# Score products of a head pair as 64-row products, with the operand B | K stored once and without zeros

## The chip, the cores and the metric

The kernel runs on one core of one Trainium2 chip. The metric is the device time of one execution in microseconds (us), taken as the median of several runs. The time before is 2406.82 us, the median of three runs (2398.74 to 2412.68).

## What is computed

One inference step of a two-layer decoder trunk: 1024 prompt tokens and 8 x 8 sample tokens, 1024 channels. Layer 0 is an HGRN2 recurrence, layer 1 an RWKV-7 recurrence; both have a memory cross-attention, a gate and an output projection. The change lies in layer 1. There, for each of 16 heads with 64 channels, the reference runs this over the tokens:

```python
def step(S, inp):
    r_t, w_t, k_t, v_t, a_t, b_t = inp
    sa = jnp.einsum('bhij,bhj->bhi', S, a_t)
    S = S * w_t[:, :, None, :] + sa[..., None] * b_t[:, :, None, :] + v_t[..., None] * k_t[:, :, None, :]
    y = jnp.einsum('bhij,bhj->bhi', S, r_t)
    return S, y
```

The kernel does it in chunks of 64 tokens. Within a chunk it needs all products of a row of B or K (with their decays, written B~ and K~) with a column of A or R (A~, R~): the scores, a 128 x 128 matrix for each head and chunk, which a mask then makes triangular.

## The kernel before

**Blocks.** Layer 1's tokens form nine blocks of the class `Blk`: eight of 128 prompt tokens (two chunks, E = 2) and one of the 64 sample tokens (E = 1); their order is RSEQ = 0, 8, 1, 2, ... (L32), so the sample block is the second. A block's 16 heads are 8 pairs. A pair owns 128 channels, which lie on the 128 partitions: head h of it on the half `HV[h]` (partitions 0 to 63, or 64 to 127). Four pairs form a group k, of which there are two.

**The parts of a block**, each a method, in the order in which a block goes through them:
- `pre` (L1399), per group: loads sg, kk, bb, k2 and r by DMA on SP's queue, a running sum G on DVE (L1425), two exponentials on ACT (L1427, L1428), then B~ | K~ into `BKz` by four products: K~ on POOL (L1432) and B~ on DVE (L1435), each once for each head, on that head's 64 partitions. A~ | R~ are made on POOL (L1440 to L1442) into `AR`.
- `score_steps` (L1457), per group, chunk and head: four products (pairs j) on TensorE into one PSUM bank `psc` (L1471), with `BKz` as the weights and `AR` as what streams; DVE multiplies the bank by the mask into `Q` (L1474). Every such product is fp32, and the trace shows it as two instructions.
- `tokens` (L1481): B~ | K~ transposed to tokens on partitions (L1499), per group and head, one instruction per chunk and pair, and a copy by ACT (L1305).
- `inverse` (L1516): a substitution on DVE in 15 steps (L1544, L1545) between copies on ACT (L1535) and DVE transposes; `merge_steps` (L1555): 32 x 32 products on TensorE (L1570) with copies on ACT and DVE.
- `chain` (L1631): the recurrence itself, with products at L1660, L1662, L1687, L1701 and L1710 (for the sample block L1657 in place of L1660); `sample_in` (L1616, products L1612 and L1627) and `sample_out` (L1746) move the sample states, `out_group` (L1776) normalises the result.

`BKz` is one tile of [128, 2 (head), 4, 4, 64] for each group (L945), made once. Channels of the other head in it are zero, set once by POOL (L948). So a product with it runs over all 128 partitions, and the zeros keep the other head's channels out. There is one `BKz` per group for all blocks: the next block's `pre` can write it when this block's `score` and `tokens` have read it.

**Banks.** `psc`, the transposes' `pbk` and (at the end) `pf` share the two banks of the pool `psm` (L1195). The merge has two banks of its own, the chain three.

**Order.** The lists PLAN and PLAN2 (L43) put the parts of the first two blocks among the last gates (products `pg`) and the memory attention. Then the loop at L1263 runs for each block n: chain(n) with high priority; values(n + 1); the merge of block n + 1 and the score of block n + 2 woven by `weave` (L1310) with `WV = (1, 2)`: one step of the merge, two of the score (one bank each), in turn; tokens and inverse of n + 2; pre of n + 3; out of n - 1. The framework then orders each engine's instructions itself, by an estimate of their times (`schedule_with_timeline_sim=True`, L1859), within what the data and priorities allow. On the chip each engine takes its instructions in the order thus fixed, so one that waits holds up those behind it.

Of the kernel before, what the change touches and what calls it, by code (L numbers as in the profile page):

```python
# [34 lines left out]
# buffers of the memory attention's tiles, by layer  # L35
XB = [2, 2]
OWB = 5
# pool of each tag of the recurrence's tiles; the others lie with the temporaries
WHERE = dict(s="s", ec="a", ecs="a", S0="l", S1="l", yv="l", o4="l", Q0="q", Q1="q", BK0="b", BK1="b")
WHERE |= {t: "t" for t in ("Ld", "Lu", "L16", "pd", "XN", "XP", "XM")}  # L40
# order of the last gates, the memory attention and the first parts of the recurrence
# [6 lines left out]
WV = (1, 2)  # L48
# [5 lines left out]
RB1 = dict(s=5, AR=6, Q=6, BKt=5, BKts=2, UV=3, UVs=2, XN=1, XP=1, W=3, S0=2, S1=2, yv=3, o4=3, ec=6, ecs=2, Sn0=2)  # L54
BF = dict(hs=3, oT=3, q=3, zn=3, lt=2, B=2, W=5, qe=1, ke=1, vv=3, cmp=2, eb=2, kt=1, S=6, oi=1, kts=1, S0=2, vx=1)
EV = 5
# banks in the heads: projections, memory attention, levels, other products of the prompt, of the sample
# [3 lines left out]
# order of the branch's channel tiles in the output projection  # L61
# [21 lines left out]
def setup(ctx, tc, g):  # L83
# [23 lines left out]
    # channel vectors as columns: [128, 128] = 16 vectors x 8 channel tiles  # L107
# [25 lines left out]
    # the token before the samples' first, as columns (batch, channel tile)  # L133
# [17 lines left out]
def sigmoid_ps(g, s, ps):  # L151
    """s = 1 / (1 + exp(-ps)) through exp and log."""
    nc = g.nc
    nc.scalar.activation(s, ps, AF.Exp, scale=-1.0)
    nc.vector.tensor_scalar(s, s, LNTOP, None, op0=ALU.min)
    nc.scalar.activation(s, s, AF.Ln, bias=1.0)
    nc.scalar.activation(s, s, AF.Exp, scale=-1.0)
# [7 lines left out]
def rstd_of(g, ss, n, scale, eps, p=128, sm=None):  # L165
    """(ss * scale + eps) ** -0.5 for a [p, n] tile."""
# [15 lines left out]
def norm_rows(g, xs, x, p):  # L182
    """xs = RMS-normalised rows (without the gain) of x [p, D]."""
# [16 lines left out]
def load_w(g, pool, src, w, kt=KT, elo="pool", raws=2):  # L200
    """hi/lo parts of src [kt * 128, w]."""
# [16 lines left out]
def gemm_cm(g, w, xh, xl, pieces, evac, m=128, c0=0):  # L218
    """out[c, t] = sum_k w[k, c] x[k, t], c on partitions; evac(ps, t0, n) per piece."""
# [10 lines left out]
def gemm_ko(g, w, xh, xl, evac):  # L230
    """As gemm_cm over all tokens, with the contraction outermost."""
# [12 lines left out]
def build_hT(g, xsrc, layer, hi, lo, sp):  # L244
    """Normed, transposed rows of the residual, as hi/lo parts [128, KT, T]."""
# [20 lines left out]
def memory_kv(g, mp, sp, kT0, v0):  # L266
    """Keys kT [128 d, XH, MEM] and values v [128 m, 2, 512] of the memory for both layers; the second's go to g.kv1.

    Also writes the two cache outputs.
    """  # L270
# [45 lines left out]
def softmax_rows(g, pool, ps, nblk, layer, rowmask=None):  # L316
    """softmax(QS * s) over the last axis of ps [128, nblk, MEM] -> SBUF tile."""
# [19 lines left out]
def cross_prompt(g, pool, q, h, kT, v, o, layer):  # L337
    """o [128, 256] = attention of head h over the memory; q [128, 256] queries."""
# [17 lines left out]
class Cross:  # L356
    """Memory attention of one layer into rows D.. of mixT, in parts: head(h) for the prompt, then sample(b) per batch."""
# [23 lines left out]
    def sample(self, bs, sp):  # L381
        """Batches bs of one group; the heads lie on the quadrants, four batches (32 tokens) form a group."""
# [70 lines left out]
def batch_masks(g):  # L453
    """bmask[(h, t32), bb] = (t32 // 8 == bb); blk[t, b] = (t mod 64 // 8 == b)."""
# [13 lines left out]
def hgrn_layer(ctx, g):  # L468
# [13 lines left out]
    # values, tokens on partitions  # L482
# [15 lines left out]
    with pool(g, "xk", 1, "right") as xk:  # L498
# [7 lines left out]
        with pool(g, "hm", 1, "right") as hm, pool(g, "h2", 1, "right") as h2, pool(g, "xc", 1, "right") as xc, \  # L506
# [13 lines left out]
            def gate(j, ms):  # L520
                """Rows 128 j.. of the branch, ms (two tiles by tokens), times silu of their gate."""
# [58 lines left out]
def hgrn_head(g, hd, wp, xh, xl, h2, hq, mbase, mlev, smask, att, atts, oT):  # L580
    """A head in two halves of the prompt's tokens, the second with the sample's."""
# [9 lines left out]
    # q = silu(z)  # L591
# [9 lines left out]
    # lt = -log f, f = sigmoid(z) (one HGRN2 layer: its lower bound lbs[0] - lbs[0] is zero)  # L601
# [20 lines left out]
def hgrn_half(g, hd, half, h2, own, mbase, mlev, smask, q, zn, lt, vv, att, atts, oT, S):  # L622
# [4 lines left out]
    # k = 1 - f = exp(zn - lt)  # L627
# [6 lines left out]
    # B = -cumulative log decay within the chunk  # L634
    B = own("B", "B")[:, :N]
    nc.vector.tensor_tensor_scan(B, smask[:, 512 * half:512 * half + N], lt, 0.0, op0=ALU.mult, op1=ALU.add)
    # two-token blocks
# [65 lines left out]
    # inter-chunk operands: qe = q exp(b), ke = k exp(b_last - b)  # L703
# [42 lines left out]
    # sample: eight batches of eight tokens  # L746
# [30 lines left out]
def hgrn_norm_out(g, h2, po, n, p, dst):  # L777
    """RMS norm over the head's value channels, then transposed into dst [128, n * p]."""
# [14 lines left out]
class NextNorm:  # L793
    """Rows of the second layer's normed input, transposed as they are made."""
# [40 lines left out]
def load_out_w(g, layer, pl, raws, ks):  # L835
    """hi/lo parts of rows of the output projection, through the pools of raws in turn."""
# [13 lines left out]
class BranchTile:  # L850
    """Gated branch of a row tile, hi/lo."""
# [21 lines left out]
def out_proj(g, layer, ws, orp, orb, done, first=None, xp=None):  # L873
    """Residual + gated branch @ w_out, rows of 128 tokens; done(i, p, x, xs) takes each row tile.

    The first layer's runs one tile later; what the last one takes is returned, its rows in pool xp.
    """
# [39 lines left out]
def rwkv_masks(g, rc, c):  # L917
    """Masks over [(s of either operand), columns of a chunk]: s < t for those of A~, s <= t for those of R~; others."""
# [18 lines left out]
    # 0 where a run of decays starts, for the scans over (pair, token)  # L937
# [6 lines left out]
    # B~ | K~ of each head, 0 in the other head's channels; per group of four pairs  # L944
    g.BKz = [rc.tile([128, 2, 4, 4, 64], F32, name=f"BKz{k}") for k in range(2)]  # L945
    for k in range(2):
        for h in range(2):
            nc.gpsimd.memset(g.BKz[k][HV[1 - h], h], 0.0)  # L948
    # inverse: identities, the lower left 16-blocks, and which 16-block a row belongs to
# [33 lines left out]
def rwkv_layer(ctx, g, nn, left):  # L983
# [13 lines left out]
    # the operands' ring of 11 slots; three of them outlive it  # L997
# [359 lines left out]


def bonus(g, pr, r, slot_):
    """Bonus weights r . (rk k) per token and head."""  # L1360
    nc = g.nc
    k2 = slot_("k2")
    nc.sync.dma_start(out=k2, in_=g.k2T[128 * pr:128 * pr + 128, :])
# [499 lines left out]
```

## Time and profile before

| | us |
|---|---|
| median of three runs | 2406.82 (2398.74 to 2412.68) |
| profiled execution, first to last instruction (span) | 2406.3 |
| mean granted TensorE clock in it | 0.942 of full speed |
| first and last score product (psc) | 1657.3 and 2137.7 |
| first and last chain product L1660 | 1804.2 and 2232.6 |

The profile gives the profiled execution by its span; no time beyond the span is listed for it. Engines are PE (TensorE products), PEld (its weight loads), DVE (VectorE), ACT (ScalarE), POOL (GpSimd), SP (SyncE, which issues DMAs). PEclk is the clock granted to TensorE as a share of full speed; its two levels are 2.4 GHz (1.0) and 1.2 GHz (0.5). "Busy" of PE counts modelled durations that overlap, so 94% busy is not 94% of what it could do. A row "x16" of the timeline merges 16 instructions of one line that follow one another; the time beside it runs from the first one's start to the last one's end.

### The profile page before, as it was taken

What the parts mean: (1) busy time and instruction counts of PE and PEld (TensorE: products, weight loads), DVE (VectorE), ACT (ScalarE), POOL (GpSimd) and SP (SyncE); (2) the same over time, 40 slices, a digit from 0 to 9 for tenths busy, and PEclk for the clock granted to TensorE, in tenths of its full rate; (3) what the DMA queues carried; (4) which work ended last, traced back from release to release, by engine and by line L of the source; (5) the groups of instructions that cost most, each with busy time, mean ns of one, the idle gap of its engine ahead of it and who ended that gap; (6) DMA issues with size and microseconds to landing.
All of it is one profiled execution on the core that took longest, in us unless ns stands there. A gap on an engine that the chain in (4) does not pass through costs nothing. (4 is left out here: it accounts for less than half of the span.)

```text
span 2406.3 us, 51073 instructions
## 1 busy us (share of the span) xinstructions
PE 2207.1 (92%) x20980; PEld 1975.4 (82%) x20981; DVE 1448.3 (60%) x2729; ACT 1080.7 (45%) x2384; POOL 947.9 (39%) x783
## 2 busy tenths in 40 slices
PE   5988999999999888997988999899999989999997
PEld 5988888877777776887988999788898978888776
DVE  6213686686788855347588403235568589795643
ACT  4223565555555543238455422344544455454421
POOL 2113564463566530013455422112224265545442
PEclk9998999999998999999999999999988799898999
DMA  5334111221443136314334343325533224323653
GB/s 183 84 95 145 37 56 49 71 62 39 105 116 108 55 108 192 115 40 166 137 128 147 122 134 115 92 58 118 153 107 95 72 79 112 88 69 94 194 161 106
DMA packets 360315, 253.02 MB, mean 105 GB/s; under 512 B 120378, under 2 KB 326402, under 8 KB 360082
## 3 DMA queue, kind: packets, MB, share of 16 engines
q1 hardware_dynamic: 348034, 237.66, 33.2%
q0 software_dynamic: 2544, 7.64, 1.0%
q10 hardware_dynamic: 9504, 4.46, 0.7%
q8 instruction: 165, 2.70, 0.5%
q14 instruction: 68, 0.56, 0.1%
HBM read 172.59 MB, written 77.11 MB: 104 GB/s over the span
## 5 line engine op out<-in xcount | busy, mean ns | idle before, releaser
L197 POOL TENSOR_TENSOR wlo<-wraw,whi 128x1024 fp32r<-128x1024 f32 (+1 forms) x84 | 217.8, 2595 | 435.5 <-ACT whi L194 421.9
L213 PE MATMUL pg<-hi,whi 128*128 128x288 f32 (+3 forms) x800 | 271.2, 339 | 13.3 <-DVE gs L532 9.3
L215 PE MATMUL pg<-hi,wlo 128*128 128x288 f32 (+3 forms) x800 | 268.1, 335 | 0.0
L214 PE MATMUL pg<-lo,whi 128*128 128x288 f32 (+3 forms) x800 | 267.1, 334 | 0.0
L213 PEld LDWEIGHTS pg<-hi,whi 128*128 128x128 f32 x800 | 156.9, 196 | 27.5 <-DVE gs L532 10.2
L194 ACT ACTIVATE whi<-wraw 128x1024 fp32r<-128x1024 f32 (+1 forms) x92 | 100.9, 1098 | 161.5 <-issue 88.4
L214 PEld LDWEIGHTS pg<-lo,whi 128*128 128x128 f32 x800 | 156.5, 196 | 12.0 <-issue 2.8
L215 PEld LDWEIGHTS pg<-hi,wlo 128*128 128x128 f32 x800 | 156.6, 196 | 11.4 <-issue 1.7
L900 PE MATMUL pout<-owh,bh 128*128 128x512 f32 (+1 forms) x432 | 142.8, 398 | 14.9 <-ACT owh L194 14.6
L900 PE MATMUL pout<-owl,bh 128*128 128x512 f32 (+1 forms) x432 | 141.5, 393 | 0.0
L900 PE MATMUL pout<-owh,bl 128*128 128x512 f32 (+1 forms) x432 | 141.0, 394 | 0.5 <-DVE bl L197 0.5
L213 PE MATMUL pg<-xhi,whi 128*128 128x384 f32 (+2 forms) x392 | 127.9, 326 | 5.7 <-DVE evs L1146 2.8
L671 POOL TENSOR_TENSOR W<-W,zn 128x256 f32<-128x256 f32 (+1 forms) x96 | 91.7, 955 | 90.2 <-ACT W L670 81.6
L215 PE MATMUL pg<-xhi,wlo 128*128 128x384 f32 (+2 forms) x392 | 126.2, 322 | 0.0
L214 PE MATMUL pg<-xlo,whi 128*128 128x384 f32 (+2 forms) x392 | 125.6, 320 | 0.0
L900 PEld LDWEIGHTS pout<-owh,bh 128*128 128x128 f32 (+1 forms) x432 | 78.8, 183 | 36.6 <-ACT owh L194 15.9
L194 ACT ACTIVATE bh<-br 128x512 fp32r<-128x512 f32 (+1 forms) x54 | 31.9, 605 | 166.0 <-POOL br L869 82.6
L197 DVE TENSOR_TENSOR bl<-br,bh 128x512 fp32r<-128x512 f32 (+1 forms) x54 | 47.1, 873 | 97.4 <-ACT bh L194 97.4
L239 PE MATMUL pg<-xhi,wlo 128*128 128x384 f32 (+1 forms) x408 | 97.2, 335 | 0.0
L900 PEld LDWEIGHTS pout<-owh,bl 128*128 128x128 f32 (+1 forms) x432 | 78.6, 182 | 21.9 <-DVE bl L197 0.9
L900 PEld LDWEIGHTS pout<-owl,bh 128*128 128x128 f32 (+1 forms) x432 | 78.9, 183 | 20.8 <-issue 0.4
L1471 PE MATMUL psc<-AR,BKz 128*128 128x128 f32 x544 | 85.6, 314 | 11.1 <-DVE Q L1474 11.1
(474 smaller groups left out, 6508.8 us busy)
## 6 DMA issues: line engine op xcount, KB each, us to landing
wraw<-in_w_in_dram SPq DMA_DIRECT2D x72, 512.0 KB
oraw<-in_w_out_dram SPq DMA_DIRECT2D x24, 512.0 KB
wraw<-in_w_mem_kv_dram SPq DMA_DIRECT2D x16, 512.0 KB
gT<-evs SPq DMA_DIRECT2D x12, 544.0 KB
vv<-vtk SPq DMA_DIRECT2D x24, 256.0 KB
br<-brT SPq DMA_DIRECT2D x24, 256.0 KB
gt<-gT SPq DMA_DIRECT2D x24, 256.0 KB
br<-mixT SPq DMA_DIRECT2D x24, 256.0 KB
```

The source lines that it names most:

```text
L194: nc.scalar.activation(hi, src, AF.Copy)
L197: (nc.gpsimd if elo == "pool" else nc.vector).tensor_sub(lo, src, hi.bitcast(F32))
L213: nc.tensor.matmul(out, ah, bh, start=first, stop=False)
L214: nc.tensor.matmul(out, ah, bl, start=False, stop=False)
L215: nc.tensor.matmul(out, al, bh, start=False, stop=last)
L239: nc.tensor.matmul(z[:, :n], a[:, k], x(k)[:, t0:t0 + n], start=first, stop=last)
L671: nc.gpsimd.tensor_mul(Wv[:, :, 0, :], Wv[:, :, 0, :], kv[:, :, 0, :])
L900: nc.tensor.matmul(ps[c][:p], a[:, k, :p], w[:, 512 * c:512 * c + 512], start=first, stop=last)
L1471: nc.tensor.matmul(ps[:, j], two(BK[:, h, j, 2 * e:2 * e + 2]), two(AR[:, j, 2 * e:2 * e + 2]), start=True, stop=True)
```

## The change

The tile of zeros is gone. B~ | K~ of a group is a tile `BK` of [128, 4, 4, 64] with each head on its own half of the partitions, and each block takes a new one: two buffers per group, `BKc0` and `BKc1`, in the pool that held `BKz` (4 x 4 KB per partition in place of 2 x 8 KB). Both heads of a group are written by one instruction on 128 partitions. A score step takes both banks at once: for each pair j the two heads' products run on partitions 0 to 63 and 64 to 127, into a bank for each head, then both masks follow. There are half as many steps, and `weave` takes one of each kind in turn. The transposes take a pair's 128 channels at once, with a bank per chunk in place of one per head. The diff also removes comments and docstrings, which are left out here.

```diff
-WHERE = dict(s="s", ec="a", ...
+WHERE = dict(BKc0="s", BKc1="s", s="s", ec="a", ...
-WV = (1, 2)
+WV = (1, 1)
-RB1 = dict(s=5, AR=6, ...
+RB1 = dict(BKc0=2, BKc1=2, s=5, AR=6, ...
...
-    g.BKz = [rc.tile([128, 2, 4, 4, 64], F32, name=f"BKz{k}") for k in range(2)]
-    for k in range(2):
-        for h in range(2):
-            nc.gpsimd.memset(g.BKz[k][HV[1 - h], h], 0.0)
...
-        BK = g.BKz[k]
+        BK = self.tile("BK", f"BKc{k}", 4, 4, 64)
+        self.BK.append(BK)
...
-        for h in range(2):
-            getattr(nc, ENG["bk0"]).tensor_mul(BK[HV[h], h, :, ri, :], v4(k2)[HV[h]], v4(En)[HV[h]])
+        getattr(nc, ENG["bk0"]).tensor_mul(BK[:, :, ri, :], v4(k2), v4(En))
         r = ld(g.rTr, "r")
-        for h in range(2):
-            getattr(nc, ENG["bk1"]).tensor_mul(BK[HV[h], h, :, ai, :], v4(bb)[HV[h]], v4(En)[HV[h]])
+        getattr(nc, ENG["bk1"]).tensor_mul(BK[:, :, ai, :], v4(bb), v4(En))
...
             for e in range(E):
+                zs = [g.psm.tile([128, 4, 128], F32, name="psc", tag="m") for _ in range(2)]
+                for j in range(4):
+                    for h in range(2):
+                        nc.tensor.matmul(zs[h][:, j], two(BK[HV[h], j, 2 * e:2 * e + 2]), two(AR[HV[h], j, 2 * e:2 * e + 2]),
+                                         start=True, stop=True)
+                m = g.rmask_s if self.sample else g.rmask[:, self.turn(e, k)]
                 for h in range(2):
-                    ps = g.psm.tile([128, 4, 128], F32, name="psc", tag="m")
-                    for j in range(4):
-                        nc.tensor.matmul(ps[:, j], two(BK[:, h, j, 2 * e:2 * e + 2]), two(AR[:, j, 2 * e:2 * e + 2]),
-                                         start=True, stop=True)
-                    m = g.rmask_s if self.sample else g.rmask[:, self.turn(e, k)]
-                    nc.vector.tensor_tensor(Q[:, e, h], ps, m[:, None].to_broadcast([128, 4, 128]), op=ALU.mult)
-                    yield
+                    nc.vector.tensor_tensor(Q[:, e, h], zs[h], m[:, None].to_broadcast([128, 4, 128]), op=ALU.mult)
+                yield
...
-            for h in range(2):
-                ps = g.psm.tile([128, E, 4, 64], F32, name="pbk", tag="m")
-                for e in range(E):
-                    for j in range(4):
-                        nc.tensor.transpose(ps[:, e, j], two(BK[HV[h], h, j, 2 * e:2 * e + 2]), g.ident[HV[h], HV[h]])
-                copy(nc, ENG["bkt"], BKt[:, :, :, HV[h]], ps)
+            for e in range(E):
+                ps = g.psm.tile([128, 4, 128], F32, name="pbk", tag="m")
+                for j in range(4):
+                    nc.tensor.transpose(ps[:, j], two(BK[:, j, 2 * e:2 * e + 2]), g.ident)
+                copy(nc, ENG["bkt"], BKt[:, e], ps)
```

## Rows read from the trace of the kernel before

**Rows 1.** The page's busy time of each engine: us, share of the span, instructions.

```profile
PE 2207.1 (92%) x20980; PEld 1975.4 (82%) x20981; DVE 1448.3 (60%) x2729; ACT 1080.7 (45%) x2384; POOL 947.9 (39%) x783
```

**Rows 2.** The table by stretches of layer 1's end: stretch in us from the span's start, its length, busy us of PE, PEld, DVE, ACT and POOL (instructions), granted clock, DMA share, GB/s.

```profile
1650.00:1790.00 140.00, 133.04 (x1319) 124.27 (x1318) 80.36 (x152) 68.25 (x158) 40.06 (x41) 0.94 0.46 129
1790.00:1930.00 140.00, 135.31 (x1922) 126.49 (x1921) 100.11 (x192) 68.19 (x165) 52.08 (x50) 0.78 0.32 83
1930.00:2070.00 140.00, 125.12 (x2186) 110.54 (x2185) 125.73 (x232) 69.51 (x174) 81.74 (x80) 0.92 0.37 97
2070.00:2170.00 100.00, 96.43 (x1680) 84.13 (x1677) 88.19 (x173) 51.71 (x135) 53.84 (x56) 0.94 0.29 76
```

**Rows 3.** The chain of waits by line, each a share of its stretch. The first row is the stretch from 1640 to 2260 us (620 us); the others are 1790 to 1930, 1930 to 2070 and 2070 to 2170 us. The rows end where the view cuts them.

```profile
by line: PE psc L1471 8.7%; PE py L1570 6.3%; PE chain L1662 5.4%; PE pn L1570 5.3%; DVE pd L1544 4.6%; PE chain L1660 4.0%; PE chain L1687 3.8%; PE pg L213 3.7%; PE pg L215 3.7%; PE pg L214 3.6%; DVE BKz L1435 3.4%; issue 2.9%; PE chain L1
...
by line: PE psc L1471 16.0%; PE pas L1627 10.0%; DVE pd L1544 8.0%; PE py L1570 6.7%; PE pn L1570 6.6%; PE chain L1662 5.5%; DVE BKz L1435 4.2%; PE chain L1657 3.6%; PE px L1570 3.3%; DVE Xc L1545 3.3%; PE pbk L1499 2.8%; DVE G L1425 2.6%; 
...
by line: DVE pd L1544 8.8%; PE py L1570 7.8%; PE psc L1471 7.1%; DVE BKz L1435 6.8%; PE chain L1660 6.5%; PE chain L1662 6.5%; issue 5.2%; PE pn L1570 5.1%; PE chain L1687 3.9%; DVE bx L1758 3.6%; ACT Ld L1535 3.4%; DVE N1p L1583 3.1%; DVE 
...
by line: PE psc L1471 12.5%; PE chain L1687 9.7%; PE py L1570 8.8%; PE chain L1662 8.8%; PE chain L1660 7.8%; PE chain L1701 7.1%; PE pn L1570 6.1%; PE chainS L1710 5.0%; DVE pd L1544 4.5%; PE px L1570 4.3%; PE pec L1767 4.2%; PE pbk L1499 
```

**Rows 4.** The instructions that write or read the banks psc: count, duration in ns (least, median, most), first and last start in us, shapes (rows*columns of weights, what streams).

```profile
L1471 PE MATMUL psc<-AR,BKz x544: 270/275/582, 1657.5 to 2137.7; 128*128 128x128 f32 x182
L1474 DVE TENSOR_TENSOR Q<-psc,rm x64: 636/682/693, 1665.7 to 2140.1; 128x512 f32<-128x512 f32 x64
L1474 DVE TENSOR_TENSOR Q<-psc,rms x4: 680/691/692, 1787.7 to 1792.2; 128x512 f32<-128x512 f32 x4
```

**Rows 5.** The score products alone (L1471) by the same stretches: length, busy us of PE and of PEld (instructions), granted clock, DMA share, GB/s; below, their sum over 600 us.

```profile
1790.00:1930.00 140.00, 34.94 (x203) 30.90 (x201) 0.78 0.32 83
...
sum 600.00, PE 85.63 PEld 76.37; mean PE 17.13 PEld 15.27
```

**Rows 6.** Score products in the timeline: start in us, us, engine, line, count [idle before, and who ended it]. The first stretch ran at half clock, the second at full clock.

```profile
1853.78 3.79 PE L1471 MATMUL psc<-AR,BKz 128*128 128x128 f32 x16 [0.81 <-DVE Q L1474]
...
1860.33 2.05 PE L1471 MATMUL psc<-AR,BKz 128*128 128x128 f32 x16
```

**Rows 7.** The timeline again, products on halves of the array at full clock: transposes of 64 rows in a prompt block (eight of one head in turn) and in the sample block (four of each head), the chain's L1710 (two columns' halves in turn) and its L1701 (one column half).

```profile
1994.05 0.71 PE L1499 MATMUL pbk<-ident,BKz 64*128 64x64 f32 x8 [0.32 <-ACT BKt L1305]
...
1794.95 0.47 PE L1499 MATMUL pbk<-ident,BKz 64*128 64x64 f32 x8
...
1797.67 0.47 PE L1499 MATMUL pbk<-ident,BKz 64*128 64x64 f32 x8
...
2142.64 0.69 PE L1710 MATMUL chainS<-UV,BKt 128*64 128x64 f32 x16
...
1867.77 1.15 PE L1701 MATMUL chain<-UV,Q 128*64 128x64 f32 x16
```

**Rows 8.** The instructions that write or read BKz and AR, columns as in Rows 4.

```profile
L1499 PE MATMUL pbk<-ident,BKz x272: 221/223/364, 1687.3 to 2153.6; 64*128 64x64 f32 x136
L1435 DVE TENSOR_TENSOR BKz<-bb,sg x36: 404/773/1774, 1513.2 to 2115.0; 64x512 f32<-64x512 f32 x32, 64x256 f32<-64x256 f32 x4
L1432 POOL TENSOR_TENSOR BKz<-k,sg x36: 722/1352/1772, 1514.0 to 2114.5; 64x512 f32<-64x512 f32 x32, 64x256 f32<-64x256 f32 x4
L948 POOL MEMSET BKz<- x4: 947/950/1116, 1484.0 to 1487.0; 64x1024 f32 x4
...
L1442 POOL TENSOR_TENSOR AR<-r,G x18: 739/1270/1724, 1652.7 to 2120.9; 128x512 f32<-128x512 f32 x16, 128x256 f32<-128x256 f32 x2
```

**Rows 9.** The timeline of DVE, and of POOL below, at 1847 to 1856 us.

```profile
1848.92 1.21 DVE L1544 TENSOR_TENSOR pd<-Xc,L 128x81 f32<-128x81 f32 x1
...
1853.95 0.31 DVE L1544 TENSOR_TENSOR pd<-Xc,L 128x144 f32<-128x144 f32 x1
...
1846.57 3.45 POOL L1432 TENSOR_TENSOR BKz<-k,sg 64x512 f32<-64x512 f32 x2 [4.90 <-ACT sg L1427]
1850.10 1.25 POOL L1440 TENSOR_TENSOR AR<-kk,G 128x504 f32<-128x504 f32 x1
```

**Rows 10.** A transpose of 128 rows in the timeline, at full clock.

```profile
2239.31 0.66 PE L1739 MATMUL pf<-ident,S 128*128 128x128 f32 x4 [0.28 <-POOL S L1716]
```

**Rows 11.** Who waited for whom from 1640 to 2260 us: us in total, times, the longest.

```profile
POOL BKz L1432 <- PE pbk L1499: 23.5, 7, 8.7
...
PE psc L1471 <- DVE Q L1474: 11.1, 5, 3.5
```

**Rows 12.** Who waited for the instructions on BKz (us, times), of the view of that tile.

```profile
  DVE BKz L1435: 4.3, 2
```

**Rows 13.** Four stretches of the sample block's stage, columns as in Rows 2.

```profile
1815.00:1835.00 20.00, 18.86 (x302) 17.36 (x302) 17.93 (x33) 10.80 (x26) 11.34 (x14) 1.00 0.29 80
1835.00:1859.00 24.00, 23.19 (x236) 21.94 (x234) 20.35 (x41) 9.49 (x23) 9.81 (x8) 0.51 0.33 89
1859.00:1876.00 17.00, 17.00 (x298) 15.76 (x297) 11.06 (x17) 11.83 (x28) 5.74 (x6) 0.99 0.32 80
1876.00:1896.00 20.00, 20.00 (x231) 18.87 (x231) 12.85 (x34) 6.67 (x16) 3.65 (x3) 0.51 0.31 80
```

More of the change, by code (lines that the diff above doesn't have):

```diff
@@ L37 @@
 OWB = 5
-WHERE = dict(s="s", ec="a", ecs="a", S0="l", S1="l", yv="l", o4="l", Q0="q", Q1="q", BK0="b", BK1="b")
+WHERE = dict(BKc0="s", BKc1="s", s="s", ec="a", ecs="a", S0="l", S1="l", yv="l", o4="l", Q0="q", Q1="q", BK0="b", BK1="b")
 WHERE |= {t: "t" for t in ("Ld", "Lu", "L16", "pd", "XN", "XP", "XM")}
@@ L53 @@
 GQ = ()
-RB1 = dict(s=5, AR=6, Q=6, BKt=5, BKts=2, UV=3, UVs=2, XN=1, XP=1, W=3, S0=2, S1=2, yv=3, o4=3, ec=6, ecs=2, Sn0=2)
+RB1 = dict(BKc0=2, BKc1=2, s=5, AR=6, Q=6, BKt=5, BKts=2, UV=3, UVs=2, XN=1, XP=1, W=3, S0=2, S1=2, yv=3, o4=3, ec=6, ecs=2, Sn0=2)
 BF = dict(hs=3, oT=3, q=3, zn=3, lt=2, B=2, W=5, qe=1, ke=1, vv=3, cmp=2, eb=2, kt=1, S=6, oi=1, kts=1, S0=2, vx=1)
@@ L1399, in pre @@
     def pre(self):
-        self.AR, self.ec = [], []
+        self.AR, self.BK, self.ec = [], [], []
         for k in range(2):
@@ L1463, in score_steps @@
         for k in range(2):
-            AR, BK = self.AR[k], g.BKz[k]
+            AR, BK = self.AR[k], self.BK[k]
             Q = self.tile("Q", f"Q{(2 * self.at + k) % 6}", 2, 2, 4, 128)
@@ L1487, in tokens @@
         for k in range(2):
-            BK = g.BKz[k]
+            BK = self.BK[k]
             if (self.i, k) == (7, 1):
```

## The prediction

> **What bounds the kernel now.** I read the page first: PE is busy 92% of the span, DVE 60%, POOL 39% [rows 1], so the question is what PE does where the change acts. All instructions on BKz and psc lie between the first pre and the last score at 2138 us, the products from 1657 us on [rows 4, 8]; so I cut that part into stretches. The reader should see two different limits there: from 1790 to 1930 us, where the sample block runs, PE is busy 135 and its weight loads 126 of 140 us, at a clock of 0.78, with DVE at 100; from 1930 to 2070 us DVE is busy 126 of 140 and PE 125 [rows 2]. PE's busy time flatters it, since a lone product counts 275 ns while sixteen in a row take 2.05 us, some 0.12 each [rows 4, 6]. So the chain of waits decides: over 1640 to 2260 us it runs through the score products for 8.7%, the largest share of any line, and through DVE's product into BKz for 3.4%. By stage the scores have 16.0, 7.1 and 12.5% [rows 3]. On 620 us that is 54 us of scores and 21 us of BKz.
>
> **The change part by part, against the profiled span of 2406.3 us.** It stands 0.5 us from the median of the runs, 2406.8, so I take the same difference for both.
>
> *Score products.* There are 34 pairs of banks (eight prompt blocks with four, the sample block with two), 272 products, 544 instructions [rows 4]. Their number stays; what changes is that two of them may run side by side on the halves of the array. The trace before has no 64-row score, so I look for other halves. Eight transposes of 64 rows take 0.71 us when one head follows itself, and 0.47 us in the sample block [rows 7]; less the 0.22 us of a single one [rows 8] that is 0.070 and 0.036 us each: two row halves at once cost half. For products that are two instructions each, L1710 alternates column halves: 16 in 0.69 us against 1.15 us for L1701, which stays on one half [rows 7]; less 0.22 us that is 0.031 and 0.062 us. So both halves of the question, rows and two-instruction products, show a factor of two, though not in one row. A bank pair now takes 2.05 us [rows 6]; less 0.275 it is 0.118 us an instruction, and with half of that it will take 0.275 + 15 x 0.059 = 1.2 us. Bounds: no gain if the halves take turns, and half of the whole 85.6 us busy [rows 5], 43 us, if every product were waited for. I take half of what lies on the chain: **-27 us**.
>
> *B~ | K~ on DVE and POOL.* Four products of 64 partitions become two of 128 for each block and group pair, K~ and B~ alike: 36 become 18 on each engine. Partitions cost nothing: 64x512 on POOL takes 1.35 us and 128x512 1.27, and DVE's 128x512 mask 0.68 against a median of 0.77 for 64x512 [rows 4, 8]. So half goes: of the 21 us of DVE on the chain **-10.5 us** (ends: 0, if the other operands are late, and -21 with the next item's wait). POOL sheds some 18 x 1.3 = 24 us; its own share of the chain is cut off in the view, so I count none. But DVE is slowed beside POOL: an inverse step on 81 elements took 1.21 us while POOL wrote BKz, one on 144 elements 0.31 us when POOL was idle [rows 9]. The inverse's 4.6% is 28 us of the chain [rows 3]; POOL's busy time of 228 us from 1650 to 2170 [rows 2] falls by a tenth, so I take **-2 us** (0 to -5).
>
> *The second buffer.* BKz is free for the next block only after score and tokens; POOL waited 23.5 us in 7 places for the transposes [rows 11] and DVE 4.3 us in 2 [rows 12]. These waits go. What is late next are the loads of sg, kk, bb, k2 and the scan, which are in the same `pre`; POOL's idle time is off the chain. 0, with ends of 0 and -4 us. SP's order of loads is not touched; r is asked for behind one POOL product in place of two, about 1.3 us earlier, and it hides as before.
>
> *Transposes.* 272 of 64 rows at 0.070 us become 136 of 128 rows, at (0.66 - 0.27) / 3 = 0.13 us [rows 10]: 19 against 18 us, 0, within 3 us either way. ACT's copies keep size and number for prompt blocks. The four memsets of 0.95 us on POOL [rows 8] lay behind layer 1's projections, which PE set; 0, and without that cover 4 us less.
>
> *The new wait.* Before, DVE emptied one bank while PE filled the other. Now a step needs both banks empty, so PE can start the next only when two masks of 0.68 us have passed [rows 4]; with the hand-overs of about 0.05 us each I count 1.5 us. Behind it on PE wait the chain's products and the merge, and behind those ACT (W) and DVE (UV). `weave` puts a part of the merge ahead of each step, and these cover the wait for the third to the ninth block of the order; the first prompt block has gates between. Uncovered I count the sample block's two steps and one more: 3 x 1.5 = **+4.5 us** (0 to 48, if 32 of 34 steps wait).
>
> The Trainium skill speaks against the change here: TensorEngine Tiling (Array Packing), Performance Considerations, says that tiling speeds up TensorE and not the emptying of PSUM, so the copies may become the bound. By it the score part would save 14 us in place of 27, and the sum below would come to -17.
>
> *The sum.* -27 - 10.5 - 2 + 4.5 = -35 us. From 1930 to 2070 us DVE stands at 126 of 140 already; its scores on the chain are 7.1% of 140, 10 us, of which I expect the half to be taken by DVE: +5. That leaves -30: **2376 us**.
>
> **The rivals.**
> *1. DVE sets the pace of the scores.* A bank costs PE about 0.93 us now and would cost 0.47; DVE needs 0.68 for its mask in any case. Where steps stand close together, the scores fall only to 0.68 / 0.93 of their 54 us, by 14. With the rest as above: -17, 2389 us. For it: DVE's 90% in one stage. Against: the weave, and 14 us less work for DVE. This is the skill's rule above in this kernel's numbers.
> *2. The clock gives it back.* Around the sample block TensorE ran at half clock from 1835 to 1859 and 1876 to 1896 us though PE was as busy as in the full-clock stretches between and before [rows 13]; the same 16 products took 3.79 us there and 2.05 at full clock [rows 6]. So the profile does not say what tips it. If less dense work moved the mean of 1790 to 1930 us from 0.78 to 0.70, its 135 us of PE would grow by 0.78 / 0.70, 15 us: -15, 2391 us.
> *3. The halves take turns.* The second instruction of a product holds the half that the first used; if the next product waited behind it, nothing would overlap. Against it is L1710 [rows 7]. Then only -10.5 - 2 + 4.5 is left: -8, 2398 us.
> *4. Slower: the wait for two banks.* The framework may order score steps one after another. PE has waited for the masks 11.1 us in 5 places already [rows 11]. Should 32 steps wait 1.5 us each, +48 us stand against the gains of 40 without the wait, and with the 5 that DVE takes it is +13: 2419 us. It decides from some 24 uncovered waits on. Against it: 28 of the 34 steps have a merge part of 64-product loops before them, and PE has other blocks' work.
>
> **How the numbers follow.** The forecast has 0.58, rival 1 0.12, rival 2 0.08, rival 3 0.07, rival 4 0.10, and 0.05 is left for a gain above the forecast's. Half a percent, 12 us, is about what a measurement of this kernel can tell from no change. Faster by more: all of the forecast and of the larger gain, most of rivals 1 and 2 (0.15): 0.78. Rival 3 and the rest of 1 and 2: 0.11 within half a percent. Slower: rival 4 and a little for an order that falls badly, 0.11. The low end takes the upper bounds: -43 for scores, -10.5, -4 without the wait, 2349, so 2350. The high end must hold rivals 1 to 3, to 2398, with a few us for their own spread: 2402. Outside lie rival 4 and the tails, 2 in 10.
>
> **What would show it.** Right: 16 score instructions in about 1.2 us at full clock, weights of 64*128; busy time of the score line near 45 us; 18 products into BK on each of DVE and POOL, of 128x512; no wait of POOL for the transposes; the scores' share of the chain halved; the end of layer 1's last product some 30 us earlier and the output projection's length unchanged. Wrong: 2 us for 16 instructions (rival 3); a long row of PE waiting for DVE's mask with count near 30 (rival 4); the sample stage at a clock of 0.70 or less (rival 2); DVE above 95% from 1930 to 2070 us (rival 1).

## The result and the profile after

The change makes the kernel slower: 2429.44 us (median of 4 runs, 2421.55 to 2442.38) against 2406.43 us, a ratio of 1.0105 with a 95% interval of [1.0079, 1.0132]. Run again beside three experiments on one chip it came to 2443.13 us against 2408.39, 1.0146 [1.0104, 1.0187]. The prediction was 2376 us, with a range of 2350 to 2402. The profiled execution took 2428.3 us, its span is 2426.5 us.

Where the two heads' score products alternate, they did what was forecast. In the timeline of the kernel after, at full clock, sixteen of them take 1.16 us, where the prediction had 1.2 and the kernel before 2.05; at half clock they take 2.09, before 3.79 [rows 6]:

```profile
1681.92 1.16 PE L1466 MATMUL psc<-AR,BK 64*128 64x128 f32 x16
1683.01 0.44 PE L215 MATMUL pg<-xhi,wlo 128*128 128x384 f32 x1
...
1839.89 2.09 PE L1466 MATMUL psc<-AR,BK 64*128 64x128 f32 x16
```

But only eight of the 34 steps ran as one row of sixteen in such a time. The framework's order split others, and where eight instructions follow one another 0.126 us apart, as one head's do, they take 1.16 us, as long as eight took before. The first line is the kernel before, the others are the kernel after, the last one at half clock:

```profile
1810.81 1.16 PE L1471 MATMUL psc<-AR,BKz 128*128 128x128 f32 x8
...
2127.40 1.16 PE L1466 MATMUL psc<-AR,BK 64*128 64x128 f32 x8
2133.23 2.08 PE L1466 MATMUL psc<-AR,BK 64*128 64x128 f32 x8 [4.67 <-DVE Q L1470]
```

So PE's busy time for scores did not halve: it is 73.8 us after and 85.6 before [rows 5], where the prediction named 45. Part of that is the lower clock. The score line by stretches, with the columns of Rows 5, first the stretches of the kernel before that Rows 5 leaves out, then the kernel after:

```profile
1650.00:1790.00 140.00, 13.97 (x87) 13.03 (x88) 0.94 0.46 129
1930.00:2070.00 140.00, 21.29 (x160) 18.92 (x160) 0.92 0.37 97
2070.00:2170.00 100.00, 15.43 (x96) 13.53 (x96) 0.94 0.29 76
...
1650.00:1790.00 140.00, 10.60 (x96) 8.98 (x96) 0.93 0.49 142
1790.00:1930.00 140.00, 24.39 (x158) 20.12 (x157) 0.66 0.29 74
1930.00:2070.00 140.00, 24.27 (x182) 20.03 (x182) 0.85 0.34 91
2070.00:2170.00 100.00, 13.37 (x104) 11.25 (x102) 0.76 0.24 63
2170.00:2250.00 80.00, 1.16 (x8) 0.96 (x8) 0.90 0.32 96
```

An estimate at full clock, each stretch's busy time multiplied by its clock, gives about 75 us before and 58 after: some 17 us saved.

The instructions on BK and its banks, with the columns of Rows 4 (L1466 answers to L1471 before, L1470 to L1474, L1494 to L1499, L1429 and L1427 to L1435 and L1432 [rows 4, 8]):

```profile
L1466 PE MATMUL psc<-AR,BK x544: 271/272/579, 1656.2 to 2172.5; 64*128 64x128 f32 x182
L1470 DVE TENSOR_TENSOR Q<-psc,rm x64: 652/680/706, 1662.5 to 2173.1; 128x512 f32<-128x512 f32 x64
...
L1494 PE MATMUL pbk<-ident,BK x136: 272/273/477, 1687.1 to 2182.3; 128*128 128x128 f32 x136
L1429 DVE TENSOR_TENSOR BK<-bb,sg x18: 412/693/1777, 1510.4 to 2123.7; 128x512 f32<-128x512 f32 x16, 128x256 f32<-128x256 f32 x2
L1427 POOL TENSOR_TENSOR BK<-k,sg x18: 731/1314/1778, 1511.2 to 2121.3; 128x512 f32<-128x512 f32 x16, 128x256 f32<-128x256 f32 x2
```

DVE and POOL have half the products, of about the same length each. Yet the last score product starts at 2172.5 us, 35 us later than before, and the chain's last product (L1655, which answers to L1660) at 2252.3 us, 20 us later, where the prediction had an end some 30 us earlier. The table by stretches tells where the reader should look, the column after POOL's busy time (granted clock; columns as in Rows 2):

```profile
1650.00:1790.00 140.00, 131.06 (x1304) 120.50 (x1303) 77.01 (x154) 70.35 (x165) 42.21 (x42) 0.93 0.49 142
1790.00:1930.00 140.00, 134.00 (x1765) 122.00 (x1764) 77.03 (x175) 59.02 (x139) 34.11 (x38) 0.66 0.29 74
1930.00:2070.00 140.00, 130.04 (x2151) 113.55 (x2148) 119.22 (x228) 72.17 (x184) 72.53 (x77) 0.85 0.34 91
2070.00:2170.00 100.00, 88.43 (x1258) 73.20 (x1256) 68.97 (x124) 42.15 (x110) 39.34 (x43) 0.76 0.24 63
```

PE is about as busy as before (only in the last stretch less, 88 us in place of 96), but from the second stretch on its clock went from 0.78 to 0.66, from 0.92 to 0.85 and from 0.94 to 0.76 [rows 2], and in the second stretch it got through 1765 instructions in place of 1922. DVE, at 100 us there before, has 77. Over the 640 us from 1640 to 2280 the clock is 0.82, where the kernel before has 0.90; with two levels, 1.0 and 0.5, that is 2 x 0.18 x 640 = 230 us at half clock against 128. The next view has two stretches of the kernel after in which the half clock held:

```profile
1820.00:1885.00 65.00, 61.51 (x714) 56.59 (x710) 33.02 (x71) 27.64 (x68) 14.10 (x14) 0.59 0.24 61
2128.00:2163.00 35.00, 30.33 (x295) 23.79 (x295) 22.48 (x42) 12.95 (x37) 7.90 (x8) 0.51 0.06 16
```

The half clock of the second began as PE came to wait 4.67 us for a DVE mask (the line at 2133.23 above): the clock is 0.98 from 2127.4 to 2128.5 us and 0.50 from 2128.6 on. PE then worked off at half clock what was queued. PE's waits for masks are no more in all than before, 8.0 us against 11.1 [rows 11]. POOL's wait for the transposes, which the prediction expected to go with the second buffer, is 18.0 us in one place, before 23.5 in 7. DVE's masks wait more for the products, 28.9 us where it was 12.9. Who waited for whom from 1640 to 2280 us in the kernel after, with the line of the kernel before last:

```profile
DVE Q L1470 <- PE psc L1466: 28.9, 15, 8.0
...
POOL BK L1427 <- PE pbk L1494: 18.0, 1, 18.0
...
PE psc L1466 <- DVE Q L1470: 8.0, 3, 4.7
...
DVE Q L1474 <- PE psc L1471: 12.9, 9, 3.8
```

In the chain of waits from 1790 to 1930 us the scores fell from 16.0% to 10.8%, not to half, while the sample states' small products (pas, 10.0% before [rows 3]) rose:

```profile
by line: PE pas L1622 14.4%; PE psc L1466 10.8%; PE py L1565 8.1%; PE pbk L1494 5.7%; ACT Ld L1530 5.4%; PE pn L1565 5.3%; PE chain L1652 4.9%; PE chain L1657 4.1%; PE ps L1607 3.6%; issue 3.3%; DMA sg<-sgw 2.8%; PE chain L1682 2.7%; DVE pd
```

### The profile page after: what moved, and what is told of

Same layout as the page of the kernel before. It is cut to its first block, busy times and chain, and to the rows that moved or that the text cites. A ratio compares the mean times of both kernels' runs of the same rounds, so it can differ in the third digit from the quotient of the medians.

```text
span 2426.5 us, 50729 instructions
## 1 busy us (share of the span) xinstructions
PE 2230.1 (92%) x20844; PEld 1987.1 (82%) x20845; DVE 1414.6 (58%) x2711; ACT 1079.8 (44%) x2382; POOL 913.9 (38%) x761
## 5 line engine op out<-in xcount | busy, mean ns | idle before, releaser
L900 PE MATMUL pout<-owh,bh 128*128 128x512 f32 (+1 forms) x432 | 143.8, 399 | 12.5 <-ACT owh L194 10.7
L239 PE MATMUL pg<-xhi,whi 128*128 128x384 f32 (+1 forms) x408 | 95.8, 334 | 0.0
```

Of the source, the lines that this page charges most:

```text
L239: nc.tensor.matmul(z[:, :n], a[:, k], x(k)[:, t0:t0 + n], start=first, stop=last)
L900: nc.tensor.matmul(ps[c][:p], a[:, k, :p], w[:, 512 * c:512 * c + 512], start=first, stop=last)
```

## The experiments

Three theories. **A**: the change lowers TensorE's clock, and the clock takes back more than it saves. **B**: the framework laid the instructions in a worse order, as any edit may. **C**: PE waits for the banks taken in pairs. The table has the median time, the ratio to the kernel before on the same chip with its interval, and the median of the runs' mean clocks; the kernel before lay between 2408 and 2411 us at 0.937 to 0.939.

| run | what it is | us | ratio | clock |
|---|---|---|---|---|
| e1 | before, products on 64 rows | 2443.9 | 1.0144 [1.0116, 1.0171] | 0.917 |
| e2 | before, banks in pairs | 2423.0 | 1.0055 [1.0035, 1.0075] | 0.935 |
| e3 | before, changed score step | 2462.0 | 1.0213 [1.0198, 1.0228] | 0.913 |
| e4 | after, with filling | 2438.5 | 1.0126 [1.0095, 1.0158] | 0.933 |
| e5 | after, on 128 rows | 2413.9 | 1.0019 [0.9998, 1.0041] | 0.938 |
| e6 | zeros in A, R, by ACT | 2412.8 | 1.0024 [1.0000, 1.0049] | 0.940 |
| e6b | the same, by POOL | 2425.5 | 1.0064 [1.0038, 1.0089] | 0.939 |
| e7 | after, one buffer | 2418.0 | 1.0059 [1.0032, 1.0087] | 0.930 |
| e8 | before, half the products | 2451.5 | 1.0184 [1.0147, 1.0221] | 0.917 |
| e9 | before, with filling | 2432.8 | 1.0107 [1.0070, 1.0144] | 0.942 |
| e10 | rest alone | 2419.6 | 1.0061 [1.0034, 1.0088] | 0.936 |
| e11 | after, again | 2443.1 | 1.0146 [1.0104, 1.0187] | 0.920 |
| n1 | before, other weave | 2408.4 | 0.9988 [0.9965, 1.0010] | 0.938 |
| n2 | before, tiny memsets | 2410.6 | 1.0002 [0.9983, 1.0021] | 0.938 |
| n3 | after, tiny memsets | 2438.2 | 1.0101 [1.0061, 1.0141] | 0.922 |
| n4 | e8 with filling | 2424.3 | 1.0064 [1.0043, 1.0085] | 0.938 |
| x1 | rest alone, one buffer | 2411.4 | 1.0007 [0.9987, 1.0026] | 0.941 |
| x2 | zeros in A, R, by DMA | 2404.2 | 0.9981 [0.9963, 0.9998] | 0.941 |

**Rows and banks apart: e1, e2, e3.** The first takes only the 64 rows:

```diff
-nc.tensor.matmul(ps[:, j], two(BK[:, h, j, 2 * e:2 * e + 2]), two(AR[:, j, 2 * e:2 * e + 2]),
+nc.tensor.matmul(ps[:, j], two(BK[HV[h], h, j, 2 * e:2 * e + 2]), two(AR[HV[h], j, 2 * e:2 * e + 2]),
```

> The kernel before, with one edit: each score product reads only its head's 64 partitions of the same tile; banks, steps, pre and transposes as before. Theory A (clock): products on half of the rows keep TensorE at its half clock for longer, and this lost the time (half clock 382 us of the profiled span after, 283 before; each half-clock microsecond costs about 0.3 us, from 2421.55 us at a clock of 0.931 and 2442.38 at 0.917, four runs of the kernel after). Then half clock rises here too, to over 330 us, and the time to 2415 to 2430 us, unless heads come to lie side by side. Theory B (order): the framework's new order of instructions with waits of PE lost it, and rows have no part: clock 0.94, 2400 to 2412 us. Theory C (pairs of banks): as B, since banks are taken one at a time here.

The second takes only the pairs of banks, `zs` and `WV = (1, 1)` of the diff, with the operands of before.

> The kernel before, with the banks taken in pairs (both heads' products in turn, then both masks; WV = (1, 1)), but still products of 128 partitions with the zeros. Theory A (clock): the clock stays at 0.94 and the time within 2400 to 2412 us. Theory C (pairs of banks): PE waits for the masks in many places; 2415 to 2430 us at a clock near 0.94. Theory B (order): anything from 2395 to 2430 us, without a link to the clock.

The third joins the two: the diff's score step on the tile with zeros.

> The kernel before, with the changed score step alone: pairs of banks, WV = (1, 1), products of 64 partitions of the tile with zeros, the two heads side by side. DVE's and POOL's products, the transposes and the single buffer stay as before. Theory A (clock): sixteen products in about 0.9 us at full clock, a clock of 0.925 or less, 2415 to 2435 us. Theory B (order): what the change lost came with the other parts' order; 2380 to 2400 us at a clock of 0.94.

The rows from 1790 to 1930 us of e1, e2 and e3 (columns as in Rows 2; before: 0.78):

```profile
1790.00:1930.00 140.00, 129.08 (x1614) 119.48 (x1610) 90.18 (x174) 58.25 (x142) 44.97 (x44) 0.62 0.30 78
```
```profile
1790.00:1930.00 140.00, 134.84 (x1971) 124.97 (x1970) 101.63 (x198) 68.39 (x168) 53.65 (x54) 0.81 0.33 84
```
```profile
1790.00:1930.00 140.00, 127.79 (x1533) 118.57 (x1531) 91.85 (x174) 56.74 (x137) 43.48 (x42) 0.59 0.31 82
```

With 64 rows the clock is 0.62 and 0.59, with 128 rows 0.81. That is A's pattern, and e1 alone lost 35 us with the banks of before, 14 us above the top of A's range. In e1, too, some products came to lie side by side (sixteen take 1.71 us at 1986.30 us, at full clock), so this edit takes time from the array and not rows alone. e3 came out 27 us above the top of A's range. The pairs of banks cost something too, 14 us at nearly the clock of before (0.935 against 0.938). A did not expect that (2400 to 2412); C did, but not for the reason it gave: in e2 PE waited 8.9 us in 6 places for the masks, the kernel before 11.1 in 5.

**Filling: e4, e9.** Ahead of the score products come products of a constant, whose results are overwritten; in e9 two for each bank of the kernel before.

```diff
+                for z in zs * 2:
+                    nc.tensor.matmul(z.rearrange("p a t -> p (a t)"), g.smask[:, :128], g.smask, start=True, stop=True)
```

> The kernel after, with four idle products of 128 x 128 x 512 in bf16 (of a constant, into the two banks that the score products then overwrite) ahead of each score step: 136 of them, 0.22 us each at full clock, 29 us of PE in all. Theory A (clock): they keep the clock up; half clock falls from 382 to below 310 us and the time to 2412 us or less although PE has more to do. Theories B and C: the added work costs 15 to 30 us, 2440 to 2460 us.

> The kernel before with 136 idle products of 128 x 128 x 512 in bf16, two ahead of each bank's score products, 29 us of PE at full clock: the control for the same filling of the kernel after, which cost 9 us while the mean clock rose from 0.922 to 0.933. If PE's time is the bound where scores are made, the time grows by 20 us or more less what the clock gives back (some 0.3 us for each half-clock microsecond): 2420 to 2435 us at 0.94 to 0.95. If PE's score time is hidden, 2400 to 2412 us.

In the kernel before the filling costs 24 us, so PE's time among the scores is not hidden: 29 us of work, 24 us of time. In the kernel after the same filling costs nothing that the two measurements of that kernel can tell (2438.5 against 2429.4 and 2443.1), while its clock rises from 0.920 or 0.922 to 0.933. The direction is A's, the size is not: 2412 us or less was missed, and from 1790 to 1930 us the clock stayed at 0.65.

**The change on whole rows: e5.** `BK[HV[h], ...]` and `AR[HV[h], ...]` become `BK[:, ...]` and `AR[:, ...]` in the diff's score step.

> The kernel after, with score products over all 128 partitions of the compact tiles: each bank gets the sum of both heads' scores, so the scores' values are wrong, and nothing else is changed: as many products, the same banks, masks, transposes and buffers. PE has more to do, since products no longer lie side by side (16 in 2.05 us in place of 1.2). Theory A (clock): half clock between 1640 and 2280 us falls from the kernel after's 225 us to 170 or less, and the time from 2429 to between 2385 and 2410 us, although PE works longer. Theory B (order or waits of the rest): the added 25 to 30 us of PE show, 2440 us or more.

PE has more to do, and the kernel takes 2413.9 us at a clock of 0.938, 15 to 29 us less than the change. B's 2440 us did not come; A's range was missed by 4 us. The same stretches as above:

```profile
1790.00:1930.00 140.00, 136.29 (x1753) 124.70 (x1752) 79.96 (x174) 59.41 (x141) 35.97 (x39) 0.72 0.29 75
1930.00:2070.00 140.00, 130.51 (x2200) 115.07 (x2200) 125.24 (x242) 75.55 (x195) 81.86 (x84) 0.93 0.37 101
2070.00:2170.00 100.00, 96.95 (x1667) 85.11 (x1668) 76.33 (x148) 50.65 (x127) 40.64 (x45) 0.92 0.25 65
```

They show that the sample block's stretch alone does not tell: its clock is 0.72 here (0.70 in e10, 0.68 in x1, both below), under the 0.78 of before, and yet the times are near that of before. What e5 has over the kernel after lies mostly in the next two stretches, 0.93 and 0.92 against 0.85 and 0.76. The stretches are cut by time, so a slower kernel has earlier work in the same one.

**Less work: e8, and filled again: n4.** This was to part the rows from the work itself.

```diff
-                    for j in range(4):
+                    for j in range(2):
...
+                    nc.vector.tensor_tensor(Q[:, e, h].rearrange("p (b j) t -> p b j t", b=2), ps[:, None, :2].to_broadcast([128, 2, 2, 128]),
+                                            m[:, None, None].to_broadcast([128, 2, 2, 128]), op=ALU.mult)
```

> The kernel before with half of the score products left out: of each bank's four pairs only two are computed, on 128 partitions with the zeros, and the mask puts them into the places of the other two as well, so pairs 2 and 3 get the scores of 0 and 1. PE's score work falls from about 62 to 31 us at full clock, as the change would have it, with no product on half the rows, no pairs of banks and nothing else changed. Theory A1 (less work on the array lowers the clock, whichever way it is saved): half clock rises from about 296 to over 340 us by the mean clock (0.93 or less), and the time comes to 2400 to 2425 us. Theory A2 (products on half of the rows lower it, whole ones don't): clock at 0.935 or more and 2375 to 2395 us, the 27 us that the prediction saw on the chain.

Half of the products gone, all on 128 rows and in single banks, and the kernel is 43 us slower, at a clock of 0.917: 1790 to 1930 us in its profile,

```profile
1790.00:1930.00 140.00, 133.78 (x1632) 123.20 (x1633) 89.91 (x179) 61.01 (x148) 46.46 (x46) 0.61 0.30 79
```

So it is not a matter of rows alone: the clock fell when score work left the array, whichever way. A1's time (up to 2425) was still too low by 26 us. n4 puts two filling products ahead of each bank of e8, the lines of e4 with `ps` for `z`:

> The kernel with half of the score products left out (2451.5 us, clock 0.917), and two idle products of 128 x 128 x 512 in bf16 ahead of each bank's products: 29 us of PE come in where 31 were left out. Pairs 2 and 3 again get the scores of 0 and 1. Theory A: the clock comes back to 0.932 or more, and the time falls to 2405 to 2430 us, with more work than the kernel it is made from. Theory B: the added work costs, 2460 us or more, at the clock of 0.917.

With 29 us more work for PE it is 27 us faster than e8, and the clock is back:

```profile
1790.00:1930.00 140.00, 129.09 (x1855) 112.33 (x1852) 97.51 (x186) 63.34 (x154) 48.03 (x48) 0.77 0.31 81
```

**Meant for the order alone: n1, n2, n3.** n1 sets `WV = (1, 1)` in the kernel before. n2 and n3 put a DVE memset of one column, `nc.vector.memset(g.nul, 0.0)`, ahead of G in each `pre_group`, of the kernel before and of the kernel after.

> The kernel before with WV = (1, 1): one step of the merge and one bank of scores in turn, in place of one and two. No work is added or taken away. It tells what a change of the instructions' order alone does. Theory A (clock, from less work on the array): clock 0.935 or more, 2400 to 2415 us. Theory B (order): up to 2430 us.

> The kernel before with one DVE memset of a single column in each group's pre, 18 in all, under 0.1 us each, some 1 to 2 us of DVE. It changes nothing else, but the framework's order of the instructions of layer 1 comes out otherwise. Theory A: clock 0.935 or more and 2400 to 2418 us. Theory B (the order of the kernel before is a lucky one, and any edit loses): 2420 to 2435 us, as after the change.

> The same memsets in the kernel after. Theory A: clock 0.915 to 0.932 again, 2420 to 2445 us. Theory B (an unlucky order): it may as well come out near 2405 us at a clock of 0.935.

The traces show no new order in any of the three. By operation and tile, n1 has all 2729 instructions of DVE, 2384 of ACT and 783 of POOL in the order of the kernel before; n2 and n3 add the 18 memsets on DVE and move nothing else there; and on PE the lists differ in 3 to 5 lines, while the profiles of the kernel after and of e11, which are one program, differ in 7. So these runs are repeats: they show that 2408 and 2411 us, and 2438 us, come again, and they do not test B.

What speaks against B is the other runs. Each of their edits did change the order on all four engines (DVE's list alone differs in 408 lines or more from that of the kernel it was made from), and over so many orders the clock still goes with the score work: 0.935 to 0.942 in the nine that keep it on whole rows or fill it up (e2, e5, e6, e6b, e9, e10, n4, x1, x2), 0.913 to 0.922 in e1, e3, e8 and the kernel after, and 0.930 and 0.933 in e7 and e4. An order that by chance lowers the clock in all of the second and none of the first is unlikely; that some of the time lost comes from the order is not excluded.

**The rest of the change: e10, e7, x1.** e10 is the kernel after with the score step of before on `BK[:, j, ...]` and `AR[:, j, ...]` and `WV = (1, 2)`; e7 is the kernel after, and x1 is e10, with `BKc0=1, BKc1=1`. e11 is the kernel after once more.

> The kernel after without the pairs of banks and without the halves: one bank at a time, WV = (1, 2), products over 128 partitions of the compact tiles, so each bank holds the sum of both heads' scores (wrong values). What is left of the change is the rest: single products of DVE and POOL, two buffers, transposes of 128 rows. By the prediction's terms this gains 10 to 15 us: 2394 to 2400 us. By the runs so far (2413.9 us with pairs of banks, and pairs of banks alone 14 us slower than the kernel before) 2398 to 2408 us at a clock of 0.938.

> The kernel after with one buffer of B | K per group in place of two. If the second buffer is worth nothing (the prediction's term of 0), the time stays within 2420 to 2440 us at a clock of 0.915 to 0.93; if the waits of POOL for the transposes counted, it comes to 2445 us or more.

> The run of the rest alone (2419.6 us: whole products over the compact tiles, one bank at a time, wrong sums of both heads), with one buffer of B | K per group in place of two. If the second buffer costs time (the kernel after came to 2418 us with one buffer and 2429 to 2443 with two), 2400 to 2412 us at a clock of 0.935 or more; if it is worth nothing either way, 2412 to 2428 us.

> The kernel after, unchanged, beside the other three on one chip, so that its time and clock can be set against theirs: 2420 to 2440 us at a mean clock of 0.917 to 0.931.

The rest gains nothing: 2419.6 us, above both ranges that were expected, and 2411.4 us with one buffer, the kernel before's time. The second buffer costs some 8 us there (the intervals, 1.0034 and up against 1.0026 and down, do not meet). In the kernel after it costs more: e7, with one buffer, takes 2418.0 us, below both of its ranges, where two buffers take 2429 to 2443. In both pairs the slower kernel has the lower clock, 0.936 against 0.941 and 0.920 or 0.922 against 0.930. And the pairs of banks that cost 14 us in e2 cost nothing here: e5 has them and takes 2413.9 us, e10 has not and takes 2419.6. So C does not explain the loss either.

**Right scores on whole rows: e6, e6b, x2.** B | K stays compact, one buffer; a chunk's A | R is copied, head by head, into one of two tiles whose other half is zero, and the products run over 128 rows, one bank at a time.

```diff
+                z = g.ARz[e if E > 1 else k]
+                for h in range(2):
+                    copy(nc, "scalar", z[HV[h], h].rearrange("p c (a t) -> p c a t", a=2), AR[HV[h], :, 2 * e:2 * e + 2])
...
+                        nc.tensor.matmul(ps[:, j], two(BK[:, j, 2 * e:2 * e + 2]), z[:, h, j], start=True, stop=True)
```

> The kernel after with products of 128 partitions that give the right scores: B | K compact as changed, with one buffer per group; ACT copies each head's half of A | R of a chunk into one of two tiles with zeros in the other half (68 copies of 64x512, about 0.6 us each, 40 us of ACT); one bank at a time and WV = (1, 2) as before. Transposes of 128 rows and single products of DVE and POOL stay. Theory A (clock): clock at 0.935 to 0.945 as in the kernel before, and the savings of DVE and POOL show: 2380 to 2405 us. If the copies on ACT hold up the scores, up to 2420 us at the same clock. Theory B: 2420 to 2440 us.

> As the run before, with the copies of A | R made by POOL in place of ACT (POOL has 24 us less to do since the change and gets some 68 copies). Theory A (clock): clock as in the kernel before; POOL's copies slow DVE, so 2395 to 2425 us. Theory B: 2420 to 2440 us.

> The kernel with zeros in A | R and right scores on 128 partitions (2412.8 us with copies by ACT), with the 68 copies made by DMA from SP's queue, so that no compute engine pays for them. If ACT's 40 us held it up, 2395 to 2408 us at a clock of 0.937 or more, which would be at or below the kernel before; if the copies wait in SP's queue ahead of the loads of the next pre, 2415 us or more.

All three have the kernel before's clock, 0.939 to 0.941. POOL's copies cost most, ACT's little, and with DMA the kernel takes 2404.2 us, 0.9981 [0.9963, 0.9998] of the kernel before. Its interval is the only one below 1, and by so little that, as one of eighteen, it does not show a gain.

## Why the prediction was wrong

**The step that failed** is the sum itself, as it was made: instructions saved, at the clock that the kernel before had been granted. It treats the clock as a property of the stretch. It is not one: e8 saves 31 us of PE at full clock by leaving products out, and loses 43. Two terms failed beside it. The score term took it that all sixteen products of a step alternate between the heads; the framework's order did not keep them so, and PE's score time fell by some 17 us at full clock. And the -12.5 us for B~ | K~, with DVE's relief from POOL, did not come even at the clock of before.

**What a half-clock microsecond costs.** Half-clock time is 2 x (1 - clock) x span. Over the 30 runs of the kernel before that stand beside e5, the time rises by 0.25 us for each (correlation 0.86). From e8 to n4, half-clock time falls from 409 to 303 us and the time by 27 us, although the filling costs 24 us by e9: (27 + 24) / 106 = 0.48 us, an estimate that takes the filling to cost the same in both and leaves the order out. The kernel after has 381 us (0.9215) against 296 (0.9385): 85 more, so 21 to 41 us, and it lost 23. Beside e11 it has 391 against 294, so 24 to 47 us, and it lost 35. So the clock can account for the loss. By the higher price the change saved 12 to 18 us beside it; by the lower price it saved nothing, and 2 to 11 us of the loss have another cause, such as the order. Which price is right stays open. e4 fits the higher one: its half-clock time is 326 us, 55 to 65 less than the kernel after's, worth 26 to 31 us at 0.48, against 24 us for the filling. What in the work on the array sets the clock was not found.

**The rivals.** Rival 2 had the mechanism and too small a size: it put the turning point at a clock of 0.70 in the sample's stage and the price at 15 us, with a chance of 0.08. The clock there was 0.66 in the first profile, and it fell by 0.07 and 0.18 in the next two stretches as well, which the rival left as they were; by e5 it is these two that count. Rival 4, the slower one, was not the cause: PE's waits for masks are 8.0 us in 3 places against 11.1 in 5 [rows 11], though e2 shows 14 us for pairs of banks that those waits do not contain. Its half-clock time, 315 us against 298, is worth 4 to 8 of them; the others stay unexplained. Rival 3 is refuted by the sixteen products in 1.16 us. Rival 1, DVE as the pace, is refuted by DVE's 119 us of 140 from 1930 to 2070 us, 85% where its sign was 95%, and by the masks, which waited for the products and not the other way round.

**The terms.** Scores: the duration was right where the heads alternate (1.16 us for 1.2), the gain of 27 us was not to be had. B~ | K~: the counts halved as said, and 12.5 us were expected of it; with whole rows e10, x1 and e5 show no gain, x1 at a clock of 0.941. The share of the chain was read as a gain, though at 3.4% of it another wait of nearly the same length can follow; which one, no run told. The second buffer: expected between 0 and -4, measured at about +8 in x1 against e10. With it the half-clock time rises from 287 to 310 us, worth 6 to 11 us, so this loss too may be the clock's; why a buffer more should lower the clock was not tried. Transposes: not measured alone. The Trainium skill, TensorEngine Tiling (Array Packing), Performance Considerations, says that the emptying of PSUM may become the bound once TensorE is faster. Here it did not: PE waited 8.0 us for the masks on DVE, and DVE 28.9 us for the products.

## What to carry to other kernels

Work taken from TensorE was worth its time here only as far as the clock held. Read the granted clock of the stretch first; where it lies between its two levels, test the gain by leaving the work out (as in e8) before rebuilding operands for it. Where products are to run side by side, look in the timeline of the kernel after whether they were left so. And before an edit counts as a test of the order alone, see in the trace that the order changed: in n1, n2 and n3 it did not, so here a loss of one per cent was never told from a shuffle by such a run.

## What was not expected of the hardware

Leaving out 31 us of products made the kernel 43 us slower, and 29 us of products of a constant, put in their place, won 27 us back; the clock of 1790 to 1930 us went 0.78, 0.61, 0.77 meanwhile, with PE busy 135, 134 and 129 of 140 us. PE's busy share thus said nothing about the clock to come. Two heads on the two halves of the rows do run at once, two-instruction fp32 products too; but the product that follows on the whole array starts late: sixteen take 1.16 us, so the last of them starts 1.16 - 0.27 = 0.89 us after the first, and the next one, at 1683.01, 0.20 us after that, where the sixteen are 0.06 us apart in the mean. It is not peculiar to the halves: in the kernel before, a product on 64 columns starts as late after the sixteen whole ones of Rows 6, 2.05 - 0.275 = 1.775 us after their first:

```profile
1860.33 2.05 PE L1471 MATMUL psc<-AR,BKz 128*128 128x128 f32 x16
1862.31 1.15 PE L1687 MATMUL chain<-W,Q 128*64 128x64 f32 x16
```
